# Reciprocal roots of a fused three-layer network: a power on GpSimd and one Newton step, in place of bit operations, a cubic and a Newton step on VectorE

## The chip, the cores and the metric

One NeuronCore of a Trainium2 chip runs the whole kernel as one program. The metric is the device time of one execution in microseconds (us). The engines are TensorE (PE in the profile, its weight loads PEld), VectorE (DVE), ScalarE (ACT) and GpSimd (POOL); SyncE (SP) issues the transfers.

## The reference, cut to what matters

Three blocks follow each other on a sequence of 256 tokens with 1024 features: a sparse-attention block, a block-attention block, and a block with window and neighbourhood attention, which ends in a retrieval of single-neuron experts. Each block normalises its input, and the attention blocks normalise queries and keys per head:

```python
def rms_norm(x, g):
    xf = x.astype(jnp.float32)
    y = xf * lax.rsqrt(jnp.mean(xf * xf, axis=-1, keepdims=True) + NORM_EPS)
    return (y * g.astype(jnp.float32)).astype(x.dtype)
...
        h = rms_norm(x, norm_g[i]) * (1 + scale[:, None, :]) + shift[:, None, :]
...
    q = partial_rope(rms_norm(q.reshape(B, S, N_HEADS, HEAD_DIM), q_g), cos, sin)
...
    return rms_norm_2(x, final_g)
```

The `lax.rsqrt` in these lines is what the change computes in another way.

## The kernel before

The 256 tokens are two tiles (t = 0, 1) of 128 partitions. Matrix products are made of three float32r matmuls each (high times high, high times low, low times high; `mm3`, lines 239 to 241). For that each weight piece of 128x512 is cast to a high part on ScalarE (line 186) and its rest is subtracted on VectorE (line 211). The program runs through layer 0 (sparse attention), layer 1 (block attention), block 2 (window and neighbourhood attention) and then `peer`, the experts: 128 tiles of `u`, a routing stage, 128 tiles of `v`, and the last norm.

Reciprocal roots are made in two helpers, both wholly on VectorE. `rsqrt` (line 243) takes 1 to 8 columns: a scaling (line 250), two integer operations that make the guess (251, 252), four for the cubic (253 to 256), three for a Newton step (257 to 259). It is called 15 times: 4 times for keys (`k_post`), 8 times for queries (`q_post`), once for the compressed keys (`cmp_kv`) and twice in `out_half` of block 2, whose result `rab` scales the products there (line 1280). `rstd_x` (line 264) takes one column in 8 instructions (271 to 278). It is called 10 times: in `norm_diag` for each token tile of the first, second, third and experts' norm, and twice at the end of `peer` (line 1577). `square` (line 261) makes the sums of squares on ScalarE, with a scale that suits the constants of the cubic.

Around a layer's norm the chain is: the products' last matmul, line 1282 (or 1280) and 1283 on VectorE (the new x), `square` on ScalarE, `rstd_x`, a diagonal matrix `diag` (line 518), the matmuls of line 525 that transpose x and scale it, then `hf`, `hh` and `hl` (lines 538 to 540, 187, 211), which are the first operand of the next layer's products. At the end of `peer`, x is `xr`: lines 1572 and 1573 add the last product, line 1576 multiplies by the gain (three of four pieces on GpSimd, the last on VectorE), `square`, `rstd_x`, and lines 1581 and 1583 scale what is written out.

The order of the instructions on each engine is not written by hand: the framework's scheduler makes it from the order of the program, from priority offsets (the numbers behind `@` in the table `ORDER`, 50 steps each) and from its own estimates of durations. Each engine then runs its list in order and waits at an instruction whose inputs aren't there. Two streams of loads share SP's queue and the DMA engines: the weights (`raw`, four buffers) and the modulation weights (`adaw`, three buffers, line 391), whose matmuls (line 396) fill gaps on TensorE. The compression weights `in_cw` (line 822), which layer 0 needs for the matmuls of line 828, come through the same queue.

GpSimd has little to do before the change: it clears the tiles `kT` (line 652), adds masks to the biases of block 2 (line 1115) and multiplies three pieces at the end (line 1576).

Of the kernel before, what the change touches and what calls it, by code (L numbers as in the profile page):

```python
# [9 lines left out]
F32 = mybir.dt.float32  # L10
F32R = mybir.dt.float32r
BF = mybir.dt.bfloat16
I32 = mybir.dt.int32
U32 = mybir.dt.uint32
AF = mybir.ActivationFunctionType
OP = mybir.AluOpType
# [4 lines left out]
D = 1024  # L21
# [4 lines left out]
EPS = 1e-6  # L26
# [123 lines left out]
class Net:  # L150
# [91 lines left out]

    def rsqrt(self, out, ss, n, mul, add, P=128):


        v = self.nc.vector
        t = self.sm.tile([128, 4, 24], F32, name="rs", tag="rs", bufs=4)
        x, y, u, w = (t[:P, i, :n] for i in range(4))
        c = (1024.0 / 27) ** 2
        v.tensor_scalar(x, ss, mul * c, add * c, op0=OP.mult, op1=OP.add)  # L250
        v.tensor_scalar(u.bitcast(I32), x.bitcast(I32), 1, None, op0=OP.arith_shift_right)
        v.tensor_scalar(y.bitcast(I32), u.bitcast(I32), -1.0, float(0x5f3759df - 2 ** 31), op0=OP.mult, op1=OP.add)
        v.tensor_tensor(u, y, y, op=OP.mult)
        v.tensor_tensor(u, u, x, op=OP.mult)
        v.scalar_tensor_tensor(w, u, -10.0 / 3, u, op0=OP.add, op1=OP.mult)
        v.scalar_tensor_tensor(w, w, 5.0, y, op0=OP.add, op1=OP.mult)
        v.tensor_tensor(u, w, w, op=OP.mult)
        v.tensor_tensor(u, u, x, op=OP.mult)
        v.scalar_tensor_tensor(out, u, -64.0 / 3, w, op0=OP.add, op1=OP.mult)

    def square(self, out, in_, sums):
        self.nc.scalar.activation(out, in_, AF.Square, scale=32.0 / 27, accum_out=sums)

    def rstd_x(self, out, s0, s1):

        v = self.nc.vector
        t = self.sm.tile([128, 4], F32, name="rx", tag="rx", bufs=2)
        x, y, u, w = (t[:, i:i + 1] for i in range(4))  # L270
        v.tensor_scalar(x, s0, s1, (32.0 / 27) ** 2 * D * EPS, op0=OP.add, op1=OP.add)
        v.tensor_scalar(u.bitcast(I32), x.bitcast(I32), 1, None, op0=OP.arith_shift_right)
        v.tensor_scalar(y.bitcast(I32), u.bitcast(I32), -1.0, float(0x5f3759df - 2 ** 31), op0=OP.mult, op1=OP.add)
        v.scalar_tensor_tensor(u, y, x, y, op0=OP.mult, op1=OP.mult)
        v.scalar_tensor_tensor(w, u, -10.0 / 3, u, op0=OP.add, op1=OP.mult)
        v.scalar_tensor_tensor(w, w, 5.0, y, op0=OP.add, op1=OP.mult)
        v.scalar_tensor_tensor(u, w, x, w, op0=OP.mult, op1=OP.mult)
        v.scalar_tensor_tensor(out, u, -64.0 / 3, w, op0=OP.add, op1=OP.mult)

    def steps(self, layer, own):  # L280

# [22 lines left out]
    def setup(self):  # L304
        nc, a = self.nc, self.a
        self.kp = self.pool("kp")
        self.hp = self.pool("hp")
        self.st = self.pool("st")
        self.nraw, self.nhl = CFG["raw"], CFG["hl"]
        self.pre = self.ctx.enter_context(ExitStack())  # L310
        self.pp = self.pool("pp", stack=self.pre, space=PSUM)
        self.nps, self.nacc = CFG["ps"], CFG["acc"]
        self.cp = self.pool("cp", stack=self.pre)
        self.sm = self.pool("sm", stack=self.pre)
        self.gp = self.pool("gp", stack=self.pre)
        cp = self.cp
        self.cc = cp.tile([128, 16], F32, name="cc")
        nc.sync.dma_start(self.cc, a["cc"])

        th = cp.tile([128, 16], F32, name="th")  # L320
        nc.scalar.activation(th, self.cc, AF.Tanh, scale=0.5)
        cs = cp.tile([128, 16], F32, name="cs")
        nc.vector.scalar_tensor_tensor(cs, th, 1.0, self.cc, op0=OP.add, op1=OP.mult)
        self.cond = cp.tile([128, 16, 32], F32, name="cond")
        nc.vector.tensor_scalar(self.cond, cs[:, :, None].to_broadcast([128, 16, 32]), 0.5, None, op0=OP.mult)
        self.cst = cp.tile([128, _CW], F32, name="cst")
        self.ident = self.kp.tile([128, 128], F32, name="ident")
        self.x = [cp.tile([128, 1024], F32, name=f"x{t}") for t in range(2)]
        self.ng = cp.tile([128, 4, 8], F32, name="ng")
        self.rows = cp.tile([128, 440], F32, name="rows")  # L330
        self.pos = cp.tile([128, 3], I32, name="pos")
        self.ona = cp.tile([128, 8], F32, name="ona")
# [1350 lines left out]
```

## Time and profile before

| | |
|---|---|
| three runs | 1389.85, 1391.97 and 1392.41 us, median 1391.97 |
| profiled execution | 1390.83 us, of which the span is 1389.1 |
| TensorE busy | 1339.5 us (96%) |
| VectorE busy | 1023.2 us (74%), 2636 instructions |
| ScalarE busy | 820.2 us (59%) |
| GpSimd busy | 21.8 us (2%), 27 instructions |
| mean granted TensorE clock | 0.99 |

Times in the rows below are microseconds from the start of the span, unless a row says ns; L250 is line 250 of the kernel. In a row of the timeline the bracket names how long the engine stood idle before it, and what ended that. The profiled execution ran in 1390.83 us, 1.14 us below the median of the three runs, and 1.73 us more than its span.

### The profile page before, as it was taken

The numbers are of one execution on the slowest core, as the hardware profiler recorded it, in microseconds if no ns is written. First come the engines' busy times: TensorE is split into PE (matmuls) and PEld (weight loads), VectorE is DVE, ScalarE is ACT, GpSimd is POOL, SyncE is SP. The second block draws the span as 40 slices with busy tenths as digits, with TensorE's granted clock in tenths as the row PEclk, the third lists the DMA queues.
The fourth block names the chain that finished last, engine by engine and source line by source line (L and its number), as shares of the span: only waits on it lengthen the run. The fifth ranks groups of instructions, "written<-read, shape, count | busy, mean of one in ns | idle before, by whom it ended". The sixth has DMA issues, their size and how long they took to land.

```text
span 1389.1 us, 25082 instructions
## 1 busy us (share of the span) xinstructions
PE 1339.5 (96%) x8842; PEld 1126.9 (81%) x8842; DVE 1023.2 (74%) x2636; ACT 820.2 (59%) x1887; POOL 21.8 (2%) x27
## 2 busy tenths in 40 slices
PE   6998999999989997999999999999999999999997
PEld 2576775587667756999999999999998888888885
DVE  3595865688576657899999868888866666677777
ACT  3354666367457664555555668888865555555554
POOL 0000000000001100000000000000000000000001
PEclk9999999999999998999999999999999999999999
DMA  8688654742586774555555575455466656667773
GB/s 302 213 283 306 218 188 149 246 157 94 207 296 204 227 236 154 173 179 179 173 180 182 168 217 177 158 166 171 158 224 209 190 192 196 197 222 242 245 242 118
DMA packets 94876, 279.17 MB, mean 201 GB/s; under 512 B 11112, under 2 KB 30320, under 8 KB 94624
## 3 DMA queue, kind: packets, MB, share of 16 engines
q1 hardware_dynamic: 94752, 277.59, 60.6%
q8 instruction: 69, 1.13, 0.3%
q14 instruction: 55, 0.45, 0.1%
HBM read 267.80 MB, written 13.94 MB: 203 GB/s over the span
## 4 chain that ended last, share of the span: by engine, by line
PE 77%; DVE 3%; DMA 2%; ACT 1%; issue 0%; ACTq 0%; DVEq 0%
PE ps L241 18%; PE ps L240 18%; PE ps L239 18%; PE ps L1501 4%; PE acc L241 3%; PE acc L240 3%; PE acc L239 3%; DMA raw<-in_w1o 1%; PE psa L396 1%; PE ps L714 1%; PE ps L525 1%; DVE lo L211 1%; PE ps L709 1%; PE ps L1125 1%; PE ps L639 1%; PE ps L1398 1%
## 5 line engine op out<-in xcount | busy, mean ns | idle before, releaser
L186 ACT CAST hi<-raw 128x512 fp32r<-128x512 f32 (+1 forms) x700 | 429.4, 618 | 350.8 <-PE ps L240 147.8
L211 DVE TENSOR_TENSOR lo<-raw,hi 128x512 fp32r<-128x512 f32 (+1 forms) x700 | 479.8, 688 | 171.2 <-ACT hi L186 158.4
L239 PE MATMUL ps<-hh,hi 128*128 128x256 f32 x1160 | 333.6, 288 | 1.2 <-DVE hh L187 1.2
L240 PE MATMUL ps<-hl,hi 128*128 128x256 f32 x1160 | 329.0, 284 | 1.1 <-DVE hl L211 1.1
L241 PE MATMUL ps<-hh,lo 128*128 128x256 f32 x1160 | 329.0, 284 | 0.0
L239 PEld LDWEIGHTS ps<-hh,hi 128*128 128x128 f32 x1160 | 223.2, 192 | 1.4 <-DVE hh L187 1.4
L240 PEld LDWEIGHTS ps<-hl,hi 128*128 128x128 f32 x1160 | 223.1, 192 | 1.3 <-DVE hl L211 1.3
L241 PEld LDWEIGHTS ps<-hh,lo 128*128 128x128 f32 x1160 | 222.9, 192 | 0.0
L239 PE MATMUL ps<-hi,Ah 128*128 128x512 f32 x508 | 198.1, 390 | 0.0
L240 PE MATMUL ps<-lo,Ah 128*128 128x512 f32 x508 | 197.7, 389 | 0.0
L241 PE MATMUL ps<-hi,Al 128*128 128x512 f32 x508 | 197.6, 389 | 0.0
L240 PEld LDWEIGHTS ps<-lo,Ah 128*128 128x128 f32 x508 | 95.4, 188 | 20.2 <-DVE lo L211 0.2
L239 PEld LDWEIGHTS ps<-hi,Ah 128*128 128x128 f32 x508 | 95.4, 188 | 19.9 <-issue 0.2
L241 PEld LDWEIGHTS ps<-hi,Al 128*128 128x128 f32 x508 | 95.3, 188 | 19.8
L1500 ACT ACTIVATE og<-o,gT 128x128 f32<-128x128 bf16 x256 | 87.2, 394 | 4.1 <-DVE o L1498 0.3
L239 PE MATMUL acc<-hi,hh 128*128 128x512 f32 (+1 forms) x176 | 69.8, 402 | 4.3 <-DVE hh L187 3.1
L240 PE MATMUL acc<-lo,hh 128*128 128x512 f32 (+1 forms) x176 | 70.6, 402 | 2.4 <-DVE lo L211 2.4
L241 PE MATMUL acc<-hi,hl 128*128 128x512 f32 (+1 forms) x176 | 70.2, 400 | 0.0
L1501 PE MATMUL ps<-og,o 128*128 128x128 f32 x512 | 65.1, 275 | 0.0
L1501 PEld LDWEIGHTS ps<-og,o 128*128 128x128 f32 x512 | 61.4, 192 | 0.0
L396 PE MATMUL psa<-adaw,cond 128*32 128x256 f32 x640 | 48.5, 390 | 4.7 <-DMA adaw<-in_adaw 4.3
L1498 DVE TENSOR_TENSOR o<-iof,eT 128x512 bf16<-128x512 f32 x64 | 44.2, 691 | 8.2 <-ACT og L1500 7.5
(397 smaller groups left out, 1937.3 us busy)
## 6 DMA issues: line engine op xcount, KB each, us to landing
raw<-in_u SPq DMA_DIRECT2D x128, 512.0 KB, 3.5
raw<-in_v SPq DMA_DIRECT2D x128, 512.0 KB, 3.5
adaw<-in_adaw SPq DMA_DIRECT2D x86, 512.0 KB, 4.8
raw<-in_w SPq DMA_DIRECT2D x48, 512.0 KB, 3.6
raw<-in_wq SPq DMA_DIRECT2D x16, 512.0 KB, 3.5
zd<-ge SPq DMA_DIRECT2D x56, 128.0 KB, 1.7
ge<-zd SPq DMA_DIRECT2D x56, 128.0 KB, 3.4
raw<-in_adaw SPq DMA_DIRECT2D x10, 512.0 KB, 3.2
```

The lines of the kernel that those rows point to most:

```text
L186: return self.nc.scalar.copy(out, in_)
L211: return self.nc.vector.tensor_tensor(lo, src, hi.bitcast(F32), op=OP.subtract)
L239: mm(out, a[0][asl], b[0][bsl], start=first, stop=False, **kw)
L240: mm(out, a[0][asl], b[1][bsl], start=False, stop=False, **kw)
L241: mm(out, a[1][asl], b[0][bsl], start=False, stop=last, **kw)
L396: i = nc.tensor.matmul(ps[32 * q:32 * q + 32, h * 256:h * 256 + 256], self.cond[:, ci + k, :], raw[:, q * 256:q * 256 + 256], start=(k == ...
L525: self.nc.tensor.matmul(ps[:, k * 128:k * 128 + 128], self.x[t][:, k4 * 512 + k * 128:k4 * 512 + k * 128 + 128], dg, start=(k == 0), stop= ...
L639: nc.tensor.transpose(pr[:P, i * 128:i * 128 + 128], s.rearrange("p a d -> p (a d)") if P == 128 else s, self.identr)
L709: nc.tensor.transpose(ps[:, r * 128:r * 128 + 128], P[a][r][:, br, kb, :], self.c("ident"))
L1498: v.tensor_tensor(o1, iob, eT[0][:, t0:t0 + 4, None].to_broadcast([128, 4, 128]), op=OP.is_equal)
L1500: nc.scalar.activation(og[:, j], o1[:, j], AF.Copy, scale=gT[:, t0 + j:t0 + j + 1])
L1501: nc.tensor.matmul(ps[:, j * 128:j * 128 + 128], o2[:, j], og[:, j], start=(j == 0), stop=(j == 3), skip_group_check=True)
```

## The change

`rsqrt` keeps its scaling (without the constant of the cubic). GpSimd then raises x to the power -1/2 (a `tensor_tensor` with the operation `pow` and a column of -0.5 that VectorE fills once at the start), and VectorE makes one Newton step in four instructions. `rstd_x` does the same with three instructions behind the power. So `rsqrt` has 5 instructions on VectorE where it had 10, and `rstd_x` 4 where it had 8, and each call has one on GpSimd. `square` takes another scale; the scratch tiles have three columns in place of four.

```diff
     def rsqrt(self, out, ss, n, mul, add, P=128):
 
-
         v = self.nc.vector
-        t = self.sm.tile([128, 4, 24], F32, name="rs", tag="rs", bufs=4)
-        x, y, u, w = (t[:P, i, :n] for i in range(4))
-        c = (1024.0 / 27) ** 2
-        v.tensor_scalar(x, ss, mul * c, add * c, op0=OP.mult, op1=OP.add)
-        v.tensor_scalar(u.bitcast(I32), x.bitcast(I32), 1, None, op0=OP.arith_shift_right)
-        v.tensor_scalar(y.bitcast(I32), u.bitcast(I32), -1.0, float(0x5f3759df - 2 ** 31), op0=OP.mult, op1=OP.add)
+        t = self.sm.tile([128, 3, 24], F32, name="rs", tag="rs", bufs=4)
+        x, y, u = (t[:P, i, :n] for i in range(3))
+        v.tensor_scalar(x, ss, mul, add, op0=OP.mult, op1=OP.add)
+        self.nc.gpsimd.tensor_tensor(y, x, self.mhalf[:P, 0:1].to_broadcast([P, n]) if n > 1 else self.mhalf[:P, 0:1], op=OP.pow)
         v.tensor_tensor(u, y, y, op=OP.mult)
         v.tensor_tensor(u, u, x, op=OP.mult)
-        v.scalar_tensor_tensor(w, u, -10.0 / 3, u, op0=OP.add, op1=OP.mult)
-        v.scalar_tensor_tensor(w, w, 5.0, y, op0=OP.add, op1=OP.mult)
-        v.tensor_tensor(u, w, w, op=OP.mult)
-        v.tensor_tensor(u, u, x, op=OP.mult)
-        v.scalar_tensor_tensor(out, u, -64.0 / 3, w, op0=OP.add, op1=OP.mult)
+        v.tensor_scalar(u, u, -0.5, 1.5, op0=OP.mult, op1=OP.add)
+        v.tensor_tensor(out, u, y, op=OP.mult)
...
     def rstd_x(self, out, s0, s1):
...
-        v.tensor_scalar(x, s0, s1, (32.0 / 27) ** 2 * D * EPS, op0=OP.add, op1=OP.add)
...
+        v.tensor_scalar(x, s0, s1, EPS, op0=OP.add, op1=OP.add)
+        self.nc.gpsimd.tensor_tensor(y, x, self.mhalf[:, 0:1], op=OP.pow)
         v.scalar_tensor_tensor(u, y, x, y, op0=OP.mult, op1=OP.mult)
...
+        v.tensor_scalar(u, u, -0.5, 1.5, op0=OP.mult, op1=OP.add)
+        v.tensor_tensor(out, u, y, op=OP.mult)
```

Since the scheduler makes the order anew, other instructions move too. In the changed program the lines behind the helpers have numbers that are 8 lower: 264 to 268 are the new `rstd_x` (265 the power on GpSimd), 510 is `diag`, 814 the load of `in_cw`, 383 that of `adaw`, 1564, 1565 and 1568 are the old 1572, 1573 and 1576.

**Place one**, SP's queue in layer 0: the loads of the compression weights (`in_cw`) among those of the modulation weights. Before:

```order
L822 DMA raw<-in_cw 128x1024
L406 DMA adar<-in_adab 32x512 x4
L391 DMA adaw<-in_adaw 128x1024
L822 DMA raw<-in_cw 128x1024
L391 DMA adaw<-in_adaw 128x1024 x4
L406 DMA adar<-in_adab 32x512
L391 DMA adaw<-in_adaw 128x1024 x2
L822 DMA raw<-in_cw 128x1024 x4
```

The same stretch in the changed program:

```order
L814 DMA raw<-in_cw 128x1024
L398 DMA adar<-in_adab 32x512 x4
L1074 DMA t5t<-in_t5t 32x8
L383 DMA adaw<-in_adaw 128x1024
L814 DMA raw<-in_cw 128x1024
L383 DMA adaw<-in_adaw 128x1024 x5
L814 DMA raw<-in_cw 128x1024 x4
```

Behind the first load shown and ahead of the last four of `in_cw` stand six loads of `adaw` where seven stood; counted from the first load by that line on, ten stand ahead of those four where thirteen stood.

**Place two**, VectorE at the norm of layer 1, second token tile: its root, its `diag`, and `hh` of the first token tile. Before:

```order
L271 TENSOR_SCALAR rx<-ssx 128x1
L272 TENSOR_SCALAR rx<-rx 128x1
L273 TENSOR_SCALAR rx<-rx 128x1
L274 SCALAR_TENSOR_TENSOR rx<-rx 128x1
L275 SCALAR_TENSOR_TENSOR rx<-rx 128x1
L276 SCALAR_TENSOR_TENSOR rx<-rx 128x1
L187 CAST hh<-hf 128x4x128
L277 SCALAR_TENSOR_TENSOR rx<-rx 128x1
L211 TENSOR_TENSOR hl<-hf,hh 128x4x128
L278 SCALAR_TENSOR_TENSOR rstd<-rx 128x1
```

In the changed program:

```order
L264 TENSOR_SCALAR rx<-ssx 128x1
L266 SCALAR_TENSOR_TENSOR rx<-rx 128x1
L267 TENSOR_SCALAR rx<-rx 128x1
L268 TENSOR_TENSOR rstd<-rx 128x1
L510 TENSOR_SCALAR diag<-ident,rstd 128x128
L187 CAST hh<-hf 128x4x128
L211 TENSOR_TENSOR hl<-hf,hh 128x4x128
```

The cast to `hh` stood inside the root; now it stands behind the whole root and behind `diag`. Line 266 waits for GpSimd.

**Place three**, VectorE at the end of the program, the roots of both token tiles. Before, from the first tile's root on:

```order
L271 TENSOR_SCALAR rx<-ss 128x1
L1573 TENSOR_TENSOR xr<-ps,xr 128x512
L272 TENSOR_SCALAR rx<-rx 128x1
L273 TENSOR_SCALAR rx<-rx 128x1
L274 SCALAR_TENSOR_TENSOR rx<-rx 128x1
L275 SCALAR_TENSOR_TENSOR rx<-rx 128x1
L1572 TENSOR_TENSOR ps<-ps,gf 128x512
L276 SCALAR_TENSOR_TENSOR rx<-rx 128x1
L1573 TENSOR_TENSOR xr<-ps,xr 128x512
L277 SCALAR_TENSOR_TENSOR rx<-rx 128x1
L1576 TENSOR_TENSOR gf<-xr,gf 128x512
```

In the changed program:

```order
L264 TENSOR_SCALAR rx<-ss 128x1
L1565 TENSOR_TENSOR xr<-ps,xr 128x512
L266 SCALAR_TENSOR_TENSOR rx<-rx 128x1
L267 TENSOR_SCALAR rx<-rx 128x1
L268 TENSOR_TENSOR rstd<-rx 128x1
L1564 TENSOR_TENSOR ps<-ps,gf 128x512
L1565 TENSOR_TENSOR xr<-ps,xr 128x512
L1568 TENSOR_TENSOR gf<-xr,gf 128x512
L264 TENSOR_SCALAR rx<-ss 128x1
L266 SCALAR_TENSOR_TENSOR rx<-rx 128x1
L267 TENSOR_SCALAR rx<-rx 128x1
```

The first tile's root now ends ahead of line 1564 of the last piece. On GpSimd the first tile's power stands ahead of the multiplication of line 1568, the second tile's behind it.

## Rows read from the trace of the kernel before

**Rows 1.** The page's first part: busy time, share of the span and instructions.

```profile
PE 1339.5 (96%) x8842; PEld 1126.9 (81%) x8842; DVE 1023.2 (74%) x2636; ACT 820.2 (59%) x1887; POOL 21.8 (2%) x27
```

**Rows 2.** Stretches: us; PE, PEld, DVE, ACT, POOL busy; PEclk; DMA share; GB/s.

```profile
60.00:100.00 40.00, 39.81 (x250) 29.93 (x249) 38.14 (x164) 20.96 (x39) 0.00 (x0) 1.00 0.74 252
...
560.00:900.00 340.00, 340.00 (x2855) 340.00 (x2855) 298.36 (x787) 209.20 (x461) 0.00 (x0) 1.00 0.56 179
```

**Rows 3.** The waits of PE: for whom, us in total, times, longest.

```profile
PE ps L525 <- DVE rx L274: 4.9, 1, 4.9
...
PE acc L239 <- DVE hh L187: 3.1, 2, 1.9
```

**Rows 4.** The tiles of the roots: times, ns (least/median/most), first and last start.

```profile
L251 DVE TENSOR_SCALAR rs<-rs x15: 140/165/569, 65.7 to 528.7; 128x8 int32<-128x8 int32 x10, 128x4 int32<-128x4 int32 x2, 128x2 int32<-128x2 int32 x2, 64x1 int32<-64x1 int32 x1
...
L274 DVE SCALAR_TENSOR_TENSOR rx<-rx x10: 212/219/1146, 13.9 to 1383.8; 128x1 f32<-128x1 f32 x10
```

**Rows 5.** POOL's groups of instructions: busy us, mean ns of one, idle before.

```profile
L1576 POOL TENSOR_TENSOR raw<-xr,gf 128x512 f32<-128x512 f32 x2 | 2.6, 1301 | 897.6 <-DVE xr L1573 897.6
...
L1673 POOL MEMSET const-uint8-127<- 128x1 uint8 x1 | 0.1, 111 | 0.0
```

**Rows 6.** Timeline of the start: start, us, engine, line; POOL's first piece of work.

```profile
0.74 1.80 POOL L652 MEMSET kT<- 64x2048 f32 x1 [0.29 <-POOLq L1673]
...
13.32 0.21 DVE L271 TENSOR_SCALAR rx<-ssx 128x1 f32<-128x1 f32 x1 [9.98 <-ACT acc L262]
...
20.84 0.68 DVE L371 TENSOR_TENSOR adar<-psa,adar 64x512 f32<-64x512 f32 x1 [3.84 <-PE psa L365]
```

**Rows 7.** Timeline of SP and of PE around the compression in layer 0.

```profile
108.55 2.55 SPq L822 DMA_DIRECT2D raw<-in_cw  x4
...
112.86 0.64 PE L396 MATMUL psa<-adaw,cond 128*32 128x256 f32 x8 [1.20 <-DMA adaw<-in_adaw]
114.15 0.71 PE L828 MATMUL ps<-raw,kcr 128*64 128x256 f32 x2 [0.65 <-DMA raw<-in_cw]
115.52 5.21 PE L828 MATMUL ps<-raw,kcr 128*64 128x256 f32 x30 [0.66 <-DMA raw<-in_cw]
```

**Rows 8.** Timeline at the norm of layer 1, second token tile.

```profile
269.19 0.21 DVE L271 TENSOR_SCALAR rx<-ssx 128x1 f32<-128x1 f32 x1 [0.58 <-ACT acc L262]
...
270.34 0.42 DVE L187 CAST hh<-hf 128x512 fp32r<-128x512 f32 x1
...
270.81 0.50 PE L239 MATMUL acc<-hi,hh 128*128 128x512 f32 x1 [1.87 <-DVE hh L187]
```

**Rows 9.** Timeline at the norm of block 2, PE.

```profile
398.71 4.93 PE L525 MATMUL ps<-diag,x 128*128 128x128 f32 x28 [0.25 <-DVE rx L276]
```

**Rows 10.** Timeline ahead of the experts: rab's root, the norm's first root.

```profile
528.06 0.16 DVE L250 TENSOR_SCALAR rs<-ssab 128x2 f32<-128x2 f32 x1
...
530.50 0.76 DVE L1280 SCALAR_TENSOR_TENSOR acc<-acc,rab,gate 128x512 f32<-128x512 f32 x1
...
537.65 0.20 DVE L271 TENSOR_SCALAR rx<-ssx 128x1 f32<-128x1 f32 x1
...
539.84 0.29 DVE L518 TENSOR_SCALAR diag<-ident,rstd 128x128 f32<-128x128 f32 x1
```

**Rows 11.** Timeline of the end.

```profile
1378.77 0.69 DVE L1573 TENSOR_TENSOR xr<-ps,xr 128x512 f32<-128x512 f32 x1
...
1379.61 1.27 POOL L1576 TENSOR_TENSOR gf<-xr,gf 128x512 f32<-128x512 f32 x1 [0.84 <-DVE rx L272]
...
1379.75 1.15 DVE L274 SCALAR_TENSOR_TENSOR rx<-rx 128x1 f32<-128x1 f32 x1
...
1381.01 0.69 DVE L1572 TENSOR_TENSOR ps<-ps,gf 128x512 f32<-128x512 f32 x1
...
1383.21 0.21 DVE L271 TENSOR_SCALAR rx<-ss 128x1 f32<-128x1 f32 x1
...
1384.74 0.16 DVE L278 SCALAR_TENSOR_TENSOR rstd<-rx 128x1 f32<-128x1 f32 x1
```

More of the change, by code (lines that the diff above doesn't have):

```diff
@@ L258, in rsqrt @@
-        v.tensor_tensor(u, u, x, op=OP.mult)
-        v.scalar_tensor_tensor(out, u, -64.0 / 3, w, op0=OP.add, op1=OP.mult)
+        v.tensor_scalar(u, u, -0.5, 1.5, op0=OP.mult, op1=OP.add)
+        v.tensor_tensor(out, u, y, op=OP.mult)
     def square(self, out, in_, sums):
-        self.nc.scalar.activation(out, in_, AF.Square, scale=32.0 / 27, accum_out=sums)
+        self.nc.scalar.activation(out, in_, AF.Square, scale=1.0 / 32.0, accum_out=sums)
     def rstd_x(self, out, s0, s1):
         v = self.nc.vector
-        t = self.sm.tile([128, 4], F32, name="rx", tag="rx", bufs=2)
@@ L270, in rstd_x @@
-        x, y, u, w = (t[:, i:i + 1] for i in range(4))
-        v.tensor_scalar(x, s0, s1, (32.0 / 27) ** 2 * D * EPS, op0=OP.add, op1=OP.add)
-        v.tensor_scalar(u.bitcast(I32), x.bitcast(I32), 1, None, op0=OP.arith_shift_right)
-        v.tensor_scalar(y.bitcast(I32), u.bitcast(I32), -1.0, float(0x5f3759df - 2 ** 31), op0=OP.mult, op1=OP.add)
+        t = self.sm.tile([128, 3], F32, name="rx", tag="rx", bufs=2)
+        x, y, u = (t[:, i:i + 1] for i in range(3))
+        v.tensor_scalar(x, s0, s1, EPS, op0=OP.add, op1=OP.add)
@@ L274, in rstd_x @@
+        self.nc.gpsimd.tensor_tensor(y, x, self.mhalf[:, 0:1], op=OP.pow)
         v.scalar_tensor_tensor(u, y, x, y, op0=OP.mult, op1=OP.mult)
[L275 to L278, printed above, removed]
+        v.tensor_scalar(u, u, -0.5, 1.5, op0=OP.mult, op1=OP.add)
@@ L325, in setup @@
         nc.vector.tensor_scalar(self.cond, cs[:, :, None].to_broadcast([128, 16, 32]), 0.5, None, op0=OP.mult)
+        self.mhalf = self.kp.tile([128, 1], F32, name="mhalf")
+        nc.vector.memset(self.mhalf, -0.5)
         self.cst = cp.tile([128, _CW], F32, name="cst")
```

## The prediction

> **What bounds the kernel now.** The page's first part comes first: TensorE is busy 96% of the span, VectorE 74%, GpSimd 2% [rows 1]. The stretches say where this matters. From 560 us on TensorE never pauses [rows 2], and no root is made between the experts' norm and the end. So only the first 560 us and the last 10 can change. Even in the stretch in which VectorE is fullest, 38.14 of 40 us, TensorE works 39.81 [rows 2]: work saved on VectorE is not time saved, unless TensorE stands behind that very instruction. The waits of TensorE tell where it does [rows 3]: 4.9 us at one place behind a root (the norm ahead of the experts), and 3.1 us behind `hh`, 1.9 of them in layer 1, next to a root. The end of the program is a chain on VectorE with a root in it. These are the places to price.
>
> **What is removed.** 15 calls lose 5 VectorE instructions each and 10 calls lose 4: 115 in all. At the median 0.165 us of such an instruction [rows 4] that is 19 us of VectorE's 1023, less one fill at the start. A dependent step costs more: the last root takes 1.69 us for 8 steps, from 1383.21 to 1384.74 + 0.16 [rows 11], so 0.21 each.
>
> **What is added.** Each root now goes VectorE, GpSimd, VectorE. Call L the time from the end of the new x to the start of the next VectorE step: a handover, the power, a handover back. No row shows a power. The nearest rows on GpSimd are a fill of one column, 0.11 us, and a product of two tiles of 512 columns, 1.30 us [rows 5]. The handover from VectorE to GpSimd at the end is 0.15 us, from 1378.77 + 0.69 to 1379.61 [rows 11]; for the way back I take the same. Ends: with a power of 0.1 and short handovers L = 0.2; with 1.5 (the long row and a little) L = 1.8. I take the middle of the two rows, 0.7, since a power is one small tile but many steps per element: L = 1.0. A root of one column then takes 0.21 + L + 3 x 0.21 = 1.84 us where it took 1.69, and a root of several columns 1.05 + L = 2.05 where ten steps took 2.1.
>
> The Trainium skill (GPSIMD Engine Reference, Performance versus the Vector engine) puts an elementwise tensor-tensor operation on GpSimd at about 2.6 cycles of a 1.2 GHz clock per element. As an estimate from that page, 8 columns are 0.02 us, L is near its low end, and the sum would be the -3.35 us below; but the page prices an addition, and no run here shows a power.
>
> **Place by place**, in the order of time, at L = 1.0 (and at 0.2 and 1.8).
>
> *Start:* 0. The two first roots stand in a row on VectorE. They begin at 13.32, and the next thing TensorE needs of VectorE starts at 20.84 [rows 6]. Two roots with their `diag` (0.29) take 2 x 2.13 = 4.3 us and end near 17.8: 3.0 us to spare.
>
> *Layer 0 and 1, the 13 roots of keys, queries and compressed keys:* 0. VectorE waits for GpSimd, and what is queued behind waits with it; of the 25 calls 10 have nothing between x and the waiting step in the new order. What hides it is TensorE's queue: in the fullest stretch four calls save 20 x 0.165 = 3.3 us of VectorE and block it at most 4 x 1.0. If that cover is gone (L = 1.8), they block 7.2, net 3.9, against 1.9 us free [rows 2]: 2 us late.
>
> *Compression weights:* -0.5 (-2.5 to 0). Ten loads of `adaw` stand ahead of the last four of `in_cw`, where thirteen stood. TensorE waited 1.20, 0.65 and 0.66 us there for loads [rows 7]. But the four are issued at 108.55, when the matmuls of the pair before are freeing `raw` buffers, and the order of the buffers has not changed. I take a fifth of the 2.5.
>
> *Layer 1:* +1.0 (+0.2, +1.8). `hh` starts at 270.34 and TensorE starts 0.47 later, having waited for it [rows 8]. It now stands behind the whole root and `diag`: 269.19 + 0.21 + L + 0.63 + 0.29 = 270.32 + L.
>
> *Block 2:* -0.2 (-0.25, +0.6). TensorE waits 0.25 us behind the interleaved roots [rows 9]. Fewer steps stand behind the last weight pieces now, and an addition of 0.7 covers most of L; what L exceeds that by is lost.
>
> *Ahead of the experts:* -0.1 (-1.25, +1.5). The root for `rab` spans 528.06 to 530.50, 2.44 us, with one subtraction of 0.65 in it [rows 10]. New: 0.21 + L + 4 x 0.21 + 0.65 = 1.70 + L, +0.26. The norm's first root spans 537.65 to 539.84, 2.19 us, with one addition of 0.65 in it [rows 10]. In the new order there are two, of which the first runs beside the power: 0.21 + L + 0.21 + 0.65 + 0.42 = 2.49, +0.30; but the second was ahead of the root before, which gives 0.65 back.
>
> *End:* +0.55 (-1.55, +2.2). The rows show GpSimd's product from 1379.61 to 1380.88, and in it the step of line 274, which took 1.15 us [rows 11] where its median is 0.219 [rows 4]: with two inputs in the local memory it stood still until GpSimd was done. In the new order the power comes ahead of that product. At L = 1.0 it ends near 1379.7, the product follows at once to 1380.97, and line 266, of the same shape, is held to 1381.0. Two steps later line 1564 starts near 1381.4 in place of 1381.01: +0.4. The last root, wholly on the path, adds 0.15. With a short power line 266 slips in ahead of the product (-0.9 and -0.65); with a long one both are late (+1.25 and +0.95).
>
> **Sum:** -0.5 + 1.0 - 0.2 - 0.1 + 0.55 = +0.75 us on the profiled execution of 1390.83. That one stands 1.14 us under the median of the runs, so the forecast is 1391.97 + 0.75 = 1392.7: no change that can be told, as two measurements of this kernel differ by about 0.2% (2.8 us) on their own. At L = 0.2 the sum is -3.35, at L = 1.8 it is +5.6 (-0.5, +1.8, +0.6, +1.5, +2.2).
>
> **The rivals.**
>
> *A long power (slower, 0.30).* Each microsecond of L beyond 1.0 costs (5.6 - 0.75) / 0.8 = 6.1 us over the four places, as it stands once in layer 1, twice ahead of the experts and twice at the end. It decides from L = 1.34 on, a power of about 1.0 us. At L = 1.8: 1397.6. For it: the product of 512 columns needs 1.30 without any function in it. Against it: no tile here has more than 8 columns.
>
> *A short power (faster, 0.14).* L = 0.2 gives 1391.97 - 3.35 = 1388.6, mostly from the end and the norm ahead of the experts. For it: the fill's 0.11 us and TensorE's 4.9 us wait behind a root. Against it: two handovers have to fit in.
>
> *The new order (0.10, half to either side).* The interleaving on TensorE, ScalarE and SP changes at about a hundred places of TensorE's list up to the experts. All three waits at the compression gone would be -2.5; the same amount lost at another load +2.5. With my other terms that gives 1390.7 or 1395.7.
>
> *The first power is late (0.06).* GpSimd is idle from 2.54 to 13.5 [rows 6], enough to get ready; if its code came only with the first call, everything beyond the 3.0 us to spare would be TensorE's. At twice the spare time that is +3.0, in all 1395.7. The Trainium skill (GPSIMD Engine Reference, Instruction dispatch) says a first call to freshly loaded code pays some 6 us that no profiled instruction shows; at that the estimate is the same +3. No run here shows it.
>
> My own forecast has the remaining 0.40, almost all within 0.2%. **Chances:** faster is the short power and half of the reordering, with a little of my own spread, 0.20; slower is the long power, part of the late first call and a little spread, 0.36; same 0.44. The range for 8 in 10 goes from 1388.2, just under the short power, to 1398.0, just over L = 1.8.
>
> **What would show it.** GpSimd gets 25 more instructions; a duration of 0.4 to 1.0 us for the power makes my L right. `hh` of layer 1 should start about 1 us behind the end of `hf`. TensorE's wait ahead of the experts should stay between 4.5 and 5.2 us, the waits at the compression between 1.5 and 2.5 in sum, and the last root should take 1.6 to 2.0 us. I am wrong if the power takes over 1 us, if TensorE shows a wait behind a root that isn't listed here, or if a load is newly waited for in layers 0 to 2.

## The result: 1.3% slower, outside the predicted range

| | before | changed |
|---|---|---|
| runs of the comparison | 1389.85 to 1392.46 us, median 1392.19 | 1408.22 to 1414.84 us, median 1410.49 |
| profiled execution | 1390.83 us, span 1389.1 | 1414.84 us, span 1412.9 |
| mean granted TensorE clock | 0.990 | 0.978 |

The ratio is 1.0128, with a 95% interval of 1.0110 to 1.0147: 18 us slower, where 0.75 was predicted and 1398.0 us was the upper end. The profiled execution of the changed kernel is the slowest of its four, so its span shows 23.8 us more and not 18.

The page's first part for the changed kernel:

```profile
PE 1353.9 (96%) x8842; PEld 1136.2 (80%) x8842; DVE 1010.4 (72%) x2522; ACT 822.0 (58%) x1887; POOL 50.0 (4%) x52
```

Against [rows 1] VectorE has 114 instructions and 12.8 us less, and GpSimd 28.2 us more. The instructions went away as forecast; of the 19 us of busy time that the prediction reckoned for them, 12.8 went. GpSimd's groups (busy us, mean ns of one) tell what they were traded for:

```profile
L249 POOL TENSOR_TENSOR rs<-rs,mhalf 128x8 f32<-128x8 f32 x10 | 18.6, 1855 | 154.4 <-DVE rs L248 101.9 <-DVE cossin L462 52.5
...
L265 POOL TENSOR_TENSOR rx<-rx,mhalf 128x1 f32<-128x1 f32 x10 | 5.5, 547 | 151.2 <-DVE rx L264 150.8 <-DVE rstd L268 0.4
...
L249 POOL TENSOR_TENSOR rs<-rs,mhalf 128x4 f32<-128x4 f32 x2 | 2.0, 1013 | 19.4 <-DVE rs L248 19.4
...
L249 POOL TENSOR_TENSOR rs<-rs,mhalf 128x2 f32<-128x2 f32 x2 | 1.4, 706 | 54.5 <-DVE rs L248 54.5
```

A power of one column takes 0.55 us, of two 0.71, of four 1.01, of eight 1.86 on average (1.64 to 2.18). VectorE's waits behind GpSimd (in total, times, longest):

```profile
DVE rs L250 <- POOL rs L249: 17.3, 14, 1.8
...
DVE rx L266 <- POOL rx L265: 4.5, 7, 0.7
```

and of TensorE's waits those that are new or have grown (`qrs` is the root of the queries, `cmpP` the weights of layer 0's compressed attention):

```profile
PE psa L388 <- DMA adaw<-in_adaw: 7.6, 9, 1.9
...
PE acc L240 <- DVE lo L211: 4.0, 6, 1.3
...
PE ps L631 <- DVE qhl L638: 2.4, 1, 2.4
...
PE ps L898 <- DVE cmpP L895: 2.0, 1, 2.0
PE ps L631 <- DVE qrs L253: 1.7, 1, 1.7
```

**Where on the way the time is lost** is read from the same event in both traces. The first of the wide roots is under way at 65.7 before [rows 4], and its power starts at 68.22 now: 2.5 us late. The second root of layer 1's norm starts at 269.19 before [rows 8] and at 286.44 now: 17.3 late. The first root ahead of the experts: 537.65 [rows 10], now 561.91, 24.3 late. The last root of all: 1383.21 [rows 11], now 1407.38, 24.2 late. So nothing is lost at the experts' norm or the end, and in this pair of traces most of it, nearly 15 us, between 68 and 286 us, in layer 0, whose roots the prediction priced at zero. (The 2.5 us at 68 us have another reason, told in the last section.)

**One place from end to end.** The timeline of the changed kernel in the fullest stretch. First a key root: scaling, power, the wait, and the rest `lo` of a weight piece that stands behind the root in VectorE's list. Then the last of the four roots, with `qhl`, the low part of the queries, behind its first step:

```profile
81.21 0.17 DVE L248 TENSOR_SCALAR rs<-kss 128x8 f32<-128x8 f32 x1
81.46 1.64 POOL L249 TENSOR_TENSOR rs<-rs,mhalf 128x8 f32<-128x8 f32 x1 [11.06 <-DVE rs L248]
83.14 0.17 DVE L250 TENSOR_TENSOR rs<-rs 128x8 f32<-128x8 f32 x1 [1.76 <-POOL rs L249]
...
83.83 0.69 DVE L211 TENSOR_TENSOR lo<-raw,hi 128x512 fp32r<-128x512 f32 x1
84.58 0.50 PE L240 MATMUL acc<-lo,hh 128*128 128x512 f32 x1 [1.29 <-DVE lo L211]
...
97.14 2.03 POOL L249 TENSOR_TENSOR rs<-rs,mhalf 128x8 f32<-128x8 f32 x1 [1.52 <-DVE rs L248]
99.20 0.17 DVE L250 TENSOR_TENSOR rs<-rs 128x8 f32<-128x8 f32 x1 [1.11 <-POOL rs L249]
99.29 0.68 DVE L638 TENSOR_TENSOR qhl<-qrow,qhl 128x512 fp32r<-128x512 f32 x1
100.12 1.23 PE L631 MATMUL ps<-identr,qhl 128*128 128x128 f32 x8 [2.43 <-DVE qhl L638]
```

From the end of the new x, 81.38, to the next step at 83.14 are 1.76 us: 0.08 of handover, 1.64 of power, 0.04 of handover back. VectorE stands still all that time; TensorE gets `lo` 1.29 us late and `qhl` 2.43 us late. And then the stretches, columns as in [rows 2]:

```profile
60.00:100.00 40.00, 36.24 (x189) 27.44 (x188) 34.86 (x146) 20.98 (x39) 7.59 (x4) 0.99 0.69 229
101.00:106.20 5.20, 5.20 (x27) 5.20 (x26) 2.44 (x8) 0.90 (x2) 0.00 (x0) 0.50 0.31 101
...
580.00:900.00 320.00, 320.00 (x2685) 320.00 (x2684) 280.19 (x755) 191.25 (x407) 0.00 (x0) 1.00 0.57 180
```

In the stretch of 60 to 100 us VectorE's busy time fell by 3.3 us against [rows 2], the saving that was counted, and TensorE's by 3.6, which was to stay; as the changed kernel runs 2.5 us late there, the two stretches don't hold quite the same work. Right behind the wait of 2.43 us the clock is granted at 0.50, that is 1.2 GHz, for the next 5.2 us; the 24 products of 256 columns behind the queries take 5.3 us there, from start to next start, and took 3.0 before. So this wait cost 2.4 us and, in this execution, another 2.3 behind it. From 580 us on TensorE is again never idle.

### The profile page after: what moved, and what is told of

Same layout as the page of the kernel before. It is cut to its first block, busy times and chain, and to the rows that moved or that the text cites. A ratio compares the mean times of both kernels' runs of the same rounds, so it can differ in the third digit from the quotient of the medians.

```text
span 1412.9 us, 24985 instructions
## 1 busy us (share of the span) xinstructions
PE 1353.9 (96%) x8842; PEld 1136.2 (80%) x8842; DVE 1010.4 (72%) x2522; ACT 822.0 (58%) x1887; POOL 50.0 (4%) x52
## 4 chain that ended last, share of the span: by engine, by line
PE 67%; DVE 1%; issue 0%; DMA 0%; ACT 0%; POOL 0%; POOLq 0%; ACTq 0%
PE ps L240 18%; PE ps L241 18%; PE ps L239 18%; PE ps L1493 4%; PE acc L241 2%; PE acc L240 1%; PE acc L239 1%; PE psa L388 1%; PE ps L1117 1%; PE ps L1390 1%; PE ps L517 0%; PE ps L631 0%; PE ps L1183 0%; DMA adaw<-in_adaw 0%; PE ps L1206 0%
```

## The experiments

Theory A: VectorE's list stands still behind each power, and a microsecond of that is about a microsecond of the kernel. Theory B: the new order of matmuls and loads costs, whatever the power takes. C blames the handovers, D the norms and the end. The waits in the table are those of one profiled execution each. e1, e7, e13 and e14 leave the reciprocal roots out, e8 leaves the cubic out: they are there for their times alone.

| kernel | ratio to before | 95% interval | VectorE waits for GpSimd, us |
|---|---|---|---|
| changed kernel | 1.0128 | 1.0110 to 1.0147 | 21.8 |
| e1, products for powers | 1.0045 | 1.0023 to 1.0067 | 3.3 |
| e2, Newton 10 later | 1.0079 | 1.0054 to 1.0103 | 18.5 |
| e3, only `rsqrt` | 1.0141 | 1.0102 to 1.0180 | 17.4 |
| e4, only the norms | 1.0013 | 0.9995 to 1.0032 | 4.6 |
| e5, two powers in `rsqrt` | 1.0297 | 1.0267 to 1.0327 | 40.9 |
| e6, Newton 40 later | 1.0089 | 1.0071 to 1.0107 | 13.6 |
| e7, nothing waits | 1.0013 | 0.9997 to 1.0028 | 0 |
| e8, bits and one Newton | 1.0042 | 1.0025 to 1.0059 | 0 |
| e9, layer 0's first four | 1.0085 | 1.0051 to 1.0118 | 4.7 |
| e10, layer 0 | 1.0080 | 1.0054 to 1.0107 | 8.1 |
| e11, layer 1 and block 2 | 1.0095 | 1.0060 to 1.0129 | 9.0 |
| e12, norms, three powers | 1.0075 | 1.0050 to 1.0101 | 15.0 |
| e13, e9 with products | 1.0042 | 1.0026 to 1.0059 | 0.3 |
| e14, e11 with products | 1.0032 | 1.0012 to 1.0051 | 0.6 |
| e15, e9 with two powers | 1.0123 | 1.0101 to 1.0146 | 11.0 |

**e1: the power's duration alone.**

```diff
-        self.nc.gpsimd.tensor_tensor(y, x, self.mhalf[...], op=OP.pow)
+        self.nc.gpsimd.tensor_tensor(y, x, self.mhalf[...], op=OP.mult)
```

The same in `rstd_x`, and the column holds 1e-6.

> GpSimd multiplies by a constant column where the changed kernel takes the power, so the reciprocal roots are left out; the list of every engine is the changed kernel's, instruction for instruction. Only the duration of GpSimd's step differs. Theory A, the long power: 1.86 us for 8 columns holds VectorE's queue (17.3 us of waits at line 250), and the rests, queries and keys behind it reach TensorE late. With a step of 0.1 to 0.4 us the waits at line 250 fall below 8 us and the time to 1390 to 1397 us. Theory B, the new order of matmuls and loads costs it whatever the power takes: 1403 to 1411 us, with the waits of TensorE for adaw loads (7.6 us) still there. Theory C, the handovers: a short step saves no more than its own length, 1402 to 1408.

1398.9 us, of the 18 us 12 gone and 6 left. In e1's waits of VectorE:

```profile
DVE rs L250 <- POOL rs L249: 1.3, 4, 0.3
```

Among e1's groups of GpSimd, the widest product:

```profile
L249 POOL TENSOR_TENSOR rs<-rs,mhalf 128x8 f32<-128x8 f32 x10 | 4.2, 420 | 156.0 <-DVE rs L248 105.3 <-DVE cossin L462 50.7
```

And among e1's waits of TensorE:

```profile
PE psa L388 <- DMA adaw<-in_adaw: 8.0, 11, 2.0
...
PE ps L898 <- DVE cmpP L895: 2.0, 1, 2.0
```

TensorE no longer waits for `qhl`, and 0.2 us in place of 1.7 for `qrs`; the waits for `adaw` and `cmpP` stand as in the changed kernel. Before the change they were

```profile
PE psa L396 <- DMA adaw<-in_adaw: 4.3, 4, 2.4
...
PE ps L906 <- DVE cmpP L903: 0.2, 1, 0.2
```

so these two alone are 5.5 us more. A is right about two thirds. C, with at least 1402, falls. B holds for what is left, as far as it is not the clock (below), and the time missed A's range by 2 us for that reason.

**e2 and e6: let VectorE do something else meanwhile.** In both the Newton steps are given a later priority, by 10 and by 40:

```diff
+        self.tc.cur_priority += 10
         v.tensor_tensor(u, y, y, op=OP.mult)
...
+        self.tc.cur_priority -= 10
```

> The four or three Newton steps behind each power get a priority 10 steps later, so that VectorE does other queued work while GpSimd computes. TensorE's list is the changed kernel's but for two pieces, the loads' list is the same, the power takes as long. Theory A: the waits at line 250 fall from 17.3 us to under 9, and the time to 1394 to 1402 us. Theory B: 1405 to 1412 us, as the matmuls and loads stand where they stood. Theory C: in between, over 1400.

> As the run with the Newton steps 10 steps later, now 40 steps. Theory A: still fewer waits of VectorE behind GpSimd than its 14.0 us (under 9), 1394 to 1401 us. If the new order of loads and matmuls costs what is left there (about 6 us, the waits for adaw and cmpP between 180 and 260 us), the time doesn't go under 1396.

1402.2 and 1402.7 us. That wins 7 and 5 of the 18 us, less than I expected; 1402.2 alone would fit theory C as well, which e1 rules out: at 10 steps later VectorE still waited 14.0 us at this line and not under 9, at 40 steps 9.1, and the second 5 us of waits brought nothing more. The keys' and queries' own results come later now, too.

**e3 and e4: which helper.** Each undoes one helper: e3 has the old `rstd_x` and `square`, e4 the old `rsqrt`. For e4:

```diff
-        v.tensor_scalar(x, ss, mul, add, op0=OP.mult, op1=OP.add)
-        self.nc.gpsimd.tensor_tensor(y, x, self.mhalf[...], op=OP.pow)
+        v.tensor_scalar(x, ss, mul * c, add * c, op0=OP.mult, op1=OP.add)
+        v.tensor_scalar(u.bitcast(I32), x.bitcast(I32), 1, None, op0=OP.arith_shift_right)
...
```

> Only the roots of keys, queries, compressed keys and block 2's scale go through the power; the ten roots of the norms are made as before. Theories A and B both put the loss into layers 0 and 1: 1404 to 1412 us. A rival D, that the norms and the end of the program carry a good part of the loss by their chains: 1396 to 1402.

> Only the ten roots of the norms (one column each, power 0.55 us) go through the power; the fifteen others are made as before, and TensorE's list is within 21 pieces of the old kernel's. Theories A and B: 1390 to 1394 us, within 0.2% of before. Rival D: 1398 to 1404.

1414.2 and 1394.2 us, 2.2 and 0.2 us above the ranges: the roots of keys, queries and block 2 carry the whole loss, the norms none that can be told. D falls.

**e5: double the wait.**

```diff
+        self.nc.gpsimd.tensor_tensor(u, x, self.mhalf[...], op=OP.pow)
         self.nc.gpsimd.tensor_tensor(y, x, self.mhalf[...], op=OP.pow)
```

> In the roots of keys, queries, compressed keys and block 2's scale GpSimd takes the power twice, the first result is thrown away; the norms' roots have one power. The loads' list is the changed kernel's, TensorE's differs in 25 pieces. Replacing the powers by products took 20.9 us of GpSimd's time out (28.1 to 7.2) and 11.6 us of the kernel's, 0.55 us for each. Theory A, powers hold VectorE's queue: the second 22.7 us add at that rate 12 us, and VectorE waits 35 to 42 us at line 251 in place of 17.3; 1417 to 1430 us. A rival: only being later than the scheduler reckoned counts, and the loss saturates: 1408 to 1415.

1434.5 us, above A's range; nothing saturates. VectorE's wait in e5:

```profile
DVE rs L251 <- POOL rs L250: 36.4, 14, 3.3
```

And TensorE's waits in e5:

```profile
PE acc L240 <- DVE lo L211: 9.5, 8, 2.9
PE ps L632 <- DVE qhl L639: 8.3, 2, 5.5
...
PE ps L632 <- DVE qrs L254: 4.4, 2, 3.3
```

Compared with the changed kernel `lo` goes from 4.0 to 9.5, `qhl` from 2.4 to 8.3 and `qrs` from 1.7 to 4.4. These are instructions that do not use the root being waited for, or, as `qrs`, stand at its end.

**e7 and e8: the saving without a wait.** In e7 the Newton steps read x in place of y, and the scaling has a factor of 1e-6:

```diff
-        v.tensor_tensor(u, y, y, op=OP.mult)
+        v.tensor_tensor(u, x, x, op=OP.mult)
...
-        v.tensor_tensor(out, u, y, op=OP.mult)
+        v.tensor_tensor(out, u, x, op=OP.mult)
```

In e8 the bit operations of the old helpers make the guess:

```diff
-        self.nc.gpsimd.tensor_tensor(y, x, self.mhalf[...], op=OP.pow)
+        v.tensor_scalar(u.bitcast(I32), x.bitcast(I32), 1, None, op0=OP.arith_shift_right)
+        v.tensor_scalar(y.bitcast(I32), u.bitcast(I32), -1.0, float(0x5f3759df - 2 ** 31), op0=OP.mult, op1=OP.add)
```

> GpSimd still makes the 25 powers, but the Newton steps read x where they read the power's result, so the roots are left out and VectorE never waits for GpSimd; VectorE's instructions are the changed kernel's in number. If the 6 us that the short product left are the new order's, 1393 to 1399 us, with TensorE waiting for adaw loads again between 180 and 260 us. If they are the handovers', 1388 to 1392, as VectorE does 115 instructions less than before.

> The guess by the two bit operations on VectorE, one Newton step behind it; the cubic is left out, and GpSimd has no part. VectorE saves 3 of 10 and 2 of 8 steps of a root, 65 instructions of 0.165 us, 10.7 us. If saved VectorE time is worth something by itself in the full stretch: 1384 to 1390 us. If not, and a new order costs by itself: 1392 to 1399.

1393.4 and 1397.6 us. e7 is the nearest to the changed kernel without its waits: all 25 powers run on GpSimd, VectorE has the changed kernel's instructions in number, and the time cannot be told from before's, though TensorE waits 6.8 us for `adaw`. So, unless two effects happen to cancel in e7's own list, neither the saving is worth anything that can be measured, nor does GpSimd's work cost anything by itself. e8 saves 65 instructions, waits for nobody, and is 0.42% slower: a new list seems to cost some microseconds or not, as it falls out.

**e9 to e11: which layer.** A count `nr` of the calls of `rsqrt` chooses between the new and the old way: 0 to 3 in e9, 0 to 6 in e10, 7 to 14 in e11; the norms are as before. The line, with the counting itself left out:

```diff
     def rsqrt(self, out, ss, n, mul, add, P=128):
+        (self.rsqrt_new if self.nr in (0, 1, 2, 3) else self.rsqrt_old)(out, ss, n, mul, add, P)
```

> Only the four roots of 8 columns of layer 0's first keys and queries, in the fullest stretch (60 to 100 us), go through the power; the eleven other roots of that helper and the norms' are made as before. VectorE's waits there should be those of the changed kernel, about 5 us. Theory A, the wait for the power is the loss, about a microsecond each: 1395 to 1400 us. The prediction's term for these four, 2 us late at the long power: 1393 to 1395.

> All seven roots of layer 0 by the power (six of 8 columns, one of one column), the rest as before. Waits of VectorE behind GpSimd 8 us (5.0 and 3.1 in the changed kernel). Theory A: 1398 to 1404 us. If layer 0 carries nearly all of the loss, as the lag at its end suggests (18.6 us): 1404 to 1411.

> The complement: the six roots of layer 1 (two of 4 columns, four of 8) and block 2's two by the power, layer 0's and the norms' as before. Waits of VectorE behind GpSimd 9.2 us (8.4 and 0.8). Theory A: 1398 to 1404 us. If layer 0 carries nearly all of the loss: 1391 to 1396.

1403.8, 1402.5 and 1405.3 us. e9 lies above both of its ranges: with the list that comes with them the four roots of 60 to 100 us cost 11 us, and layer 0's three others add none. Layer 1 and block 2 cost as much, so "nearly all in layer 0" falls too; the lag in one pair of traces had misled me. The two parts add up to more than e3; each comes with a list of its own, so they need not add up.

**e12: the norms with a long power.** The old `rsqrt`, and in `rstd_x`:

```diff
+        self.nc.gpsimd.tensor_tensor(u, x, self.mhalf[:, 0:1], op=OP.pow)
+        self.nc.gpsimd.tensor_tensor(u, x, self.mhalf[:, 0:1], op=OP.pow)
         self.nc.gpsimd.tensor_tensor(y, x, self.mhalf[:, 0:1], op=OP.pow)
```

> Only the ten roots of the norms, each with three powers in a row on GpSimd, two of them thrown away, so that VectorE is without the result for about 1.9 us; TensorE's list is within 5 pieces of the old kernel's. By the prediction's prices for the norms and the end at 1.8 us (layer 1 +1.8, block 2 +0.6, about +0.7 ahead of the experts without block 2's scale, end +2.2): 5 us, 1395 to 1399 us. If each wait of a norm costs its full length, as those of keys and queries do, ten by about 1.1 us over the single power: 1401 to 1407. If they are hidden: 1390 to 1394.

1402.1 us. VectorE's wait for a norm's power in e4:

```profile
DVE rx L272 <- POOL rx L271: 4.6, 7, 0.7
```

The same in e12:

```profile
DVE rx L274 <- POOL rx L272: 15.0, 10, 1.8
```

10.4 us more of waits are 8.6 us more of time (1.0075 against 1.0013). The time lies in the range for waits that cost their full length, above the 1395 to 1399 us of the prediction's own prices. The norms are cheap in the changed kernel because a power of one column is short, not because they are covered.

**e13 to e15: wait or order, at a fixed list.** e13 and e14 are e9 and e11 with e1's edit, e15 is e9 with e5's.

> The run with only layer 0's first four key and query roots on GpSimd (1403.8 us), each with a product by a constant in place of the power, so those four roots are left out; the list of every engine is the same. Theory A, the wait: the waits of VectorE fall from 4.7 to under 1 us, the time to 1392 to 1397. Theory B, the new order: 1399 to 1404.

> The run with only layer 1's and block 2's eight roots on GpSimd (1405.3 us), with products in place of the powers, so those eight roots are left out; the list of every engine is the same. Theory A: the waits fall from 9.0 to under 1.5 us, the time to 1391 to 1397. Theory B: 1400 to 1406.

> The run with only layer 0's first four key and query roots on GpSimd, each with two powers in a row, the first thrown away; TensorE's list differs in 3 pieces. Each wait grows by 1.63 us, 6.5 in all. Theory A at one microsecond for one: 1409 to 1414 us. Theory B: 1402 to 1406.

1399.4, 1397.9 and 1411.1 us. e13 lies at the lower end of B's range, e14 between the two, e15 in A's range: both are at work. Of TensorE's waits in e9:

```profile
PE ps L923 <- DVE cmpP L920: 2.5, 1, 2.5
PE ps L656 <- DVE qhl L663: 2.4, 1, 2.4
```

In e13 only the first of them is left:

```profile
PE ps L923 <- DVE cmpP L920: 2.5, 1, 2.5
```

The wait for `qhl` goes with the power, the one for `cmpP` stays with the list (it was 0.2 us before the change).

**The price of a wait**, from the pairs whose lists are the same or nearly so, time by the ratios times 1392 us: changed kernel against e1 11.6 us for 18.5 us of waits; e9 against e13 6.0 for 4.4; e11 against e14 8.8 for 8.4; e12 against e4 8.6 for 10.4; e15 against e9 5.3 for 6.3; e5 against the changed kernel 23.5 for 19.1. The lists of the first three pairs are identical; on TensorE those of the others differ in some 20, 2 and 25 places, and e12's differs from e4's on VectorE as well. That is 0.6 to 1.4 us of time for each of waiting, around one; each difference has some microseconds of noise (by the medians e9 against e13 is 4.4 us and e15 against e9 7.3). **The price of the list** is what is left where a product takes the power's place: 6.3 us in e1, 5.8 in e13, 4.5 in e14, with the product (0.2 us and more) and the handovers still in it.

**The clock's share** can be bounded from the mean clock of every execution: one minus it, times the span, is the most that the lower level, half the upper one, can have cost. On average this is 16 to 17 us in the executions of the kernel before that ran beside e1 to e15, 22.9 in the changed kernel, 20.8 in e1, 20.2 in e13, 19.3 in e14 and 35.4 in e5. So up to 6 or 7 of the changed kernel's 18 us may be clock, and 3 to 5 us of what was just put down to the list in e1, e13 and e14. Executions at one clock say more: at 0.987 the changed kernel took 1408.22 and 1408.60 us, the kernel before 1391.7 to 1395.2 in seven, about 15 us less; at 0.988 and 0.989 e1 took 1394.5 to 1395.9 us in three, the kernel before 1389.2 to 1394.7 in the five beside it, about 4 us less. Most of the loss is there at equal clock, and some of the list's price too. With the clock's most taken off, the six pairs above leave 0.4 to 1.1 us for each microsecond of waiting.

No version beat the kernel before.

## Why the prediction was wrong

*What failed: "Layer 0 and 1, the 13 roots of keys, queries and compressed keys: 0".* Two things in that step. First, one L for all column counts, with the reason that no tile has more than 8 columns. A power costs 0.155 us more for each column (0.55, 0.71 and 1.01 us for one, two and four), which makes 1.63 us at 8; it took 1.64 us where VectorE stood still and 1.86 on average, and L was 1.76 and more, the long end that I had kept for a rival. Second, the cover. The step set 3.3 us of saved VectorE time against the waits and let TensorE's queue hide the rest; at L = 1.8 it made 2 us of the four roots, and e9 against e13 shows 6.0 (4.4 by the medians). VectorE's list is in order, and in that stretch it hands TensorE a `lo` or a `qhl` all the time; what stands behind a waiting step reaches TensorE late by the wait, whether VectorE has work saved elsewhere or not. e7 says what the saving was worth there: nothing that shows.

*The rivals.* The long power (0.30) had the right mechanism and sign, but was priced at the four norm-like places alone, where the powers turned out short: 1397.6 us were its time, 1410.5 came. At those places its prices were too low besides: in e12, with three powers in a row, the norms cost 10 us against before and not 5. The new order (0.10) was real as well and up to twice as dear as the 2.5 us written down: its place was not the compression but `adaw` and `cmpP` further on in layer 0. The late first call did not happen: by GpSimd's timeline the first power ran at 13.42 us as fast as the later ones. The second line, from the instructions of line 265, shows why that proves little:

```profile
13.42 0.54 POOL L265 TENSOR_TENSOR rx<-rx,mhalf 128x1 f32<-128x1 f32 x1 [10.89 <-DVE rx L264]
...
L265 POOLq MODIFY_POOL_CONFIG  x2: 4/4/4, 2.5 to 2.5; - x2
```

GpSimd's sequencer ran line 265's two `MODIFY_POOL_CONFIG` at 2.5 us, and then the engine was idle until the power, 10.89 us in all. The Trainium skill (GPSIMD Engine Reference, Instruction dispatch) has a first call to freshly loaded code pay about 6 us, counted from such an instruction; this case's first power took 0.54 us and VectorE went on at 13.99, so a load of that length would have been over by then, and no run here shows whether there was one. The Trainium skill's rule for elementwise work (GPSIMD Engine Reference, Performance versus the Vector engine), from which 0.02 us for 8 columns had been estimated, does not give the time of tiles this small: the product took 0.20 us at the least and 0.42 on average (e1), and the power 1.86.

*Start: 0* came out right: the two roots and their `diag` end at 16.63 us (the prediction's own sum, 13.32 and 4.3, is 17.6 and not 17.8), and VectorE is not needed until 20.83. *Compression weights: -0.5*: TensorE waited 0.28, 0.63, 1.61 and 0.68 us for loads there, 3.2 in all where it was 2.5 [rows 7]: +0.7, where the bounds were -2.5 and 0.

*Layer 1: +1.0* did not come. VectorE's timeline at the second token tile of layer 1's norm, then TensorE's:

```profile
288.22 0.42 DVE L187 CAST hh<-hf 128x512 fp32r<-128x512 f32 x1
...
288.45 2.02 PE L517 MATMUL ps<-diag,x 128*128 128x128 f32 x16 [0.99 <-DVE diag L510]
290.23 0.47 PE L239 MATMUL acc<-hi,hh 128*128 128x512 f32 x1
```

`hh` does stand behind the whole root now, but TensorE waits for `diag` instead (0.99 us here and 1.15 for the first token tile) and finds `hh` ready; before it waited 0.31 for the first `diag` and 1.87 for `hh`, so both come to 2.1 or 2.2 us. *Block 2: -0.2* was right for the root, which nobody waits for any more; a load of `adaw` is waited for there, 1.89 us at 418.87, as one was before (2.35 us at 397.82).

*Ahead of the experts: -0.1.* Better than that, by VectorE's timeline and, last, TensorE's:

```profile
553.41 0.17 DVE L248 TENSOR_SCALAR rs<-ssab 128x2 f32<-128x2 f32 x1
554.39 0.16 DVE L250 TENSOR_TENSOR rs<-rs 128x2 f32<-128x2 f32 x1 [0.81 <-POOL rs L249]
...
555.66 1.42 DVE L1272 SCALAR_TENSOR_TENSOR acc<-acc,rab,gate 128x512 f32<-128x512 f32 x2
...
561.91 0.20 DVE L264 TENSOR_SCALAR rx<-ssx 128x1 f32<-128x1 f32 x1
...
563.88 0.29 DVE L510 TENSOR_SCALAR diag<-ident,rstd 128x128 f32<-128x128 f32 x1
...
564.31 6.74 PE L517 MATMUL ps<-diag,x 128*128 128x128 f32 x32 [3.58 <-DVE diag L510]
```

The root of `rab` takes 2.25 us (2.44 before, 2.70 predicted), the norm's first 1.97 (2.19, 2.49), and TensorE waits 3.58 us where it waited 4.94 [rows 3] (4.5 to 5.2 predicted). L was 0.81 at the first and 0.66 at the second, not 1.0.

*End: +0.55.* From line 1573, now 1565, to line 1572, now 1564, were 2.24 us [rows 11] and are 2.04; the last root takes 1.47 and not 1.69, by VectorE's timeline of the end:

```profile
1403.14 0.69 DVE L1565 TENSOR_TENSOR xr<-ps,xr 128x512 f32<-128x512 f32 x1
...
1404.31 0.95 DVE L268 TENSOR_TENSOR rstd<-rx 128x1 f32<-128x1 f32 x1
1405.18 0.69 DVE L1564 TENSOR_TENSOR ps<-ps,gf 128x512 f32<-128x512 f32 x1
...
1407.38 0.21 DVE L264 TENSOR_SCALAR rx<-ss 128x1 f32<-128x1 f32 x1
1408.25 0.22 DVE L266 SCALAR_TENSOR_TENSOR rx<-rx 128x1 f32<-128x1 f32 x1 [0.66 <-POOL rx L265]
...
1408.69 0.16 DVE L268 TENSOR_TENSOR rstd<-rx 128x1 f32<-128x1 f32 x1
```

So -0.4 us. With a power of 0.54 us line 266 slips in ahead of GpSimd's product, as forecast for a short power; the step that stands still until the product is done is now line 268 (0.95 us).

Six of the seven terms were off by no more than about 1.5 us, though the layer-1 term did not come and the compression's and the end's came with the other sign; at none of the four norm places did a root cost more than forecast. The one left at zero held the result. The tests I had set say so: "wrong if the power takes over 1 us, if TensorE shows a wait behind a root that isn't listed here": both came, and so did the third, a load newly waited for in layers 0 to 2 (`adaw`, nine waits where there were four).

*What stays open.* How much of the loss, within the bounds above, is TensorE's clock. By its means the clock took at most (1 - 0.978) x 1412.9 = 31.1 us from the profiled execution, and at most 13.9 from the one before, so up to 17 of the 23.8 us between these two; less, as TensorE also stood idle at the low clock. In the changed kernel's other runs, at 0.983 to 0.987, it is less. Such stretches stand behind waits, but not behind each (below). What in a new list costs the microseconds that are left at equal clock was read from TensorE's waits alone and not tested by a run. Why layer 0's last three roots cost nothing on top of the first four was not tried further either.

## What to carry to other kernels

A step that is moved to another engine leaves a wait in the list of the engine it came from, and everything behind it in that list comes later by the wait: ask who takes the next results of that engine, not how many instructions it saves. Price the moved step for each of its sizes, and where the scheduler makes the order, keep some microseconds for the new list itself. The quickest test is the one of e1 and e7: the same list with a cheap step in place, and the same steps with nobody waiting.

## What was not expected of the hardware

The power on GpSimd costs by columns, 0.39 + 0.155 for each in us up to 4; at 8 columns its second call in a row took 1.63 us (e5), which is on that line, and the first 1.86 on average. The difference goes with what VectorE does meanwhile: at 81.46 us, where VectorE stood still, a power of 8 columns took 1.64 us in the changed kernel, and the longest, beside VectorE's work,

```profile
68.22 2.18 POOL L249 TENSOR_TENSOR rs<-rs,mhalf 128x8 f32<-128x8 f32 x1 [52.55 <-DVE cossin L462]
```

A product of 8 columns took 0.20 us at the same place and 0.74 at this one (e1). So at these two places the step on GpSimd took 0.54 us longer beside a busy VectorE; which of VectorE's instructions do that was not tested.

TensorE's clock fell in the changed kernel ahead of any wide root. TensorE's timeline at the start has matmuls of one shape on either side of it (0.40 and 0.63 us):

```profile
27.34 0.40 PE L241 MATMUL acc<-hi,hl 128*128 128x512 f32 x1
...
28.89 0.79 PE L240 MATMUL acc<-lo,hh 128*128 128x512 f32 x1 [0.83 <-DVE lo L211]
29.48 0.63 PE L241 MATMUL acc<-hi,hl 128*128 128x512 f32 x1
```

The waits ahead were 1.25, 0.77 and 0.83 us; before the change they were 1.26, 0.77 and 0.92 at the same places, and the clock held. At 27.4 us the two traces are level; the matmuls of the second norm (line 525, now 517) start at 50.06 before and at 52.56 now, so these are the 2.5 us that are lost by 68 us. In the same way the wait of 2.43 us for `qhl` was followed by 5.2 us at 1.2 GHz in the changed kernel, while in e9 the wait of 2.39 us at the same place was not, and the 24 products behind it took 3.0 us. A wait of TensorE has a price that is not in its own length, and one execution doesn't show whether it is paid.
